# Three buffers of exponentials, banded attention in pairs of blocks, and a half-precision output projection in a hybrid decoder layer

## The chip, the cores and the metric

The kernel runs on one core of a Trainium2 chip. The metric is device time in microseconds (us) of one execution. Engine names are those of the profile: PE multiplies matrices (PEld is its weight load), DVE works on vectors, ACT evaluates functions, POOL is the general engine, SP issues transfers.

## The reference

One decoder layer over 2048 tokens of width 1024 with two attention branches that share one normalised input and one input projection:

```
h    = rms_norm(x, g_pre) * (1 + scale) + shift          # scale, shift, gate from c
proj = h @ w_in  ->  qa ka va fa za (branch A)  qb kb vb zb (branch B)
A: 8 heads of 64, causal softmax attention over all keys, with cumulative
   log-forget gates added to the scores ("FoX")
B: 8 query heads, 2 key heads, rotary positions, window of 128 keys,
   a learned sink logit per head
oa, ob = A * silu(za), B * silu(zb)
y    = concat(oa, ob) @ w_out
out  = x + gate * rms_norm(y, g_post)
```

The inputs and the output are float32. The kernel therefore splits most operands into a high and a low half-precision part and multiplies high x high, high x low and low x high into one sum.

## The kernel before, in words

The order of the work on every engine is written out by hand (`tc.manual_schedule`). Each engine runs its own instructions in the order in which the code issues them. Two helpers spread the work. `fill(n)` issues the next n *units*: a unit is usually three PE products (high x high, high x low, low x high of one slice of 128 rows of the contraction). `after(k, f)` puts f aside, and the k-th call of `tick()` issues it: so an evacuation by ACT or DVE is issued some units after the PE work that it reads. `tick2()` ticks at every second call.

1. *Start* (to about 150 us): modulation vectors from c, normalisation of x, its transpose `hT` in two f16 parts.
2. *Banded stage* (branch B, about 156 to 450 us). 64 `Window` objects, one for each pair of query heads j (4) and block of 128 queries i (16). For each: `scores` (PE, six products 64 rows high, the two heads side by side, L822, into a PSUM tile of one buffer), `maxima` (DVE, L834, which also writes the masked scores to SBUF; POOL copies the sink beside them), `exps` (ACT, L843, two of 257 columns), `turn` (PE, four float32 transposes, L852; ACT and DVE then form the halves, L861 and L857) and `pv` (PE, twelve products, L870; DVE scales them, POOL stores to `o_d`). Between these the loop places the units of the input projection: 296 units over the 64 windows. The four steps of a window are spread over the turns of the loop: scores(n+1) are in the middle of turn n, its transposes at the start of turn n+2.
3. *FoX stage* (branch A, to about 1083 us). Heads 0 to 7, each in 20 *steps* of up to 1024 columns (two key blocks by 512 queries; steps on the diagonal are narrower). Step s: `exp32` (ACT, L1211, reads the scores in PSUM, writes a float32 tile from pool `fxp`, two buffers), `high` (ACT, L1215, f16 copy in a tile from `fxh`, four buffers), `low` (DVE, L1218, the remainder, issued a step later), the scores of step s+1 (PE, L1204 to L1207, one PSUM tile), and `pv` of step s-2 (PE, L1228 to L1231). Between them stand units of the input projection (heads 0 to 6), and `munits`: products and DVE maxima that bound the scores of the next queries (L1156, L1159, L1161), with `ext` rows through PE and ACT (L1123, L1124).
   In head 7 there is no input projection left. Steps 0 to 7 load w_out in 16 pieces, two a step (L1279, from a pool of three buffers), and steps 1 to 8 split them (ACT L1285, DVE L1286) into `wohl`. From step 8 on the first two blocks of the output run as filler (36 units, `N_IN`).
4. *Output* (to the end). 16 blocks of 128 tokens, class `Out`: `turn` in two halves (four transposes each, L1309; DVE multiplies by the gate z, L1313; ACT makes the high part, L1314; DVE the low part, L1315), `product` (three PE products for each of 8 slices and two column halves, L1328), an evacuation (ACT squares, L1337; DVE scales, L1338), and `store` (root of the mean square by DVE, L1347 and L93 to L107; scaling and adding x, L1353; store, L1354). Here both operands are of type float32r, split as high and low of that type.

Of the kernel before, what the change touches and what calls it, by code (L numbers as in the profile page):

```python
# [11 lines left out]
F32R = mybir.dt.float32r  # L12
# [7 lines left out]
P = 128  # L20
S = 2048
D = 1024
# [19 lines left out]
def hybrid_layer(  # L42
# [66 lines left out]


# [38 lines left out]
    snk = const.tile([P, 8], F32, name="snk")  # L149
    mz = const.tile([1, 1], F32, name="mz")  # L150
# [102 lines left out]
    scl, isc, czs, facs, kaps = {}, {}, {}, {}, {}  # L253
# [4 lines left out]
    def w_done(key):  # L258
# [13 lines left out]
        elif kind == "va":  # L272
            kaps[key] = kappa(pw, key)
        else:
            czs[key] = col(f"cz_{key}")
            V.tensor_scalar(czs[key][:], pw[:], pH[:], 2.0 ** -29, op0=ALU.mult, op1=ALU.mult)
            facs[key] = col(f"fac_{key}")
            V.tensor_tensor(facs[key][:], kaps["vb" if kind == "zb" else f"va{j}"][:], czs[key][:], op=ALU.mult)
# [390 lines left out]
    onp = swa_pool("onp", 4)  # L669
# [136 lines left out]
    class Window:  # L806


        def __init__(self, j, i):
            self.j, self.i, self.g = j, i, j // 2  # L810
            self.k0 = max(i - 1, 0)
            self.w = (i + 1 - self.k0) * P
            self.nk = self.w // P

        def scores(self):
            w, i = self.w, self.i
            self.pss = ps_s.tile([P, 2, CH], F32, tag="s", name="pss")
            q, qo = ab[self.j, i // 4], (i % 4) * P
            for n, (a, b) in enumerate(((0, 0), (0, 1), (1, 0))):
                for h in range(2):  # L820
                    r = slice(64 * h, 64 * h + 64)
                    PE.matmul(self.pss[:, h, :w], q[r, a, qo:qo + P],  # L822
                              kst[self.g][r, b, self.k0 * P:(i + 1) * P], start=(n == 0), stop=(n == 2))

        def maxima(self):
            w, moff = self.w, 2 * P - self.w
# [3 lines left out]
            self.sm_ = sws.tile([P, 2, 2 * P + 1], F32, tag="ss", name="sm_")  # L830
            G.tensor_copy(self.sm_[:, :, w:w + 1], snk2.unsqueeze(2))
            m = sm(2, "b_m")
            for h in range(2):
                V.tensor_tensor_reduce(self.sm_[:, h, :w], self.pss[:, h, :w], bmask[:, moff:], scale=scl[key][:],  # L834
                                       scalar=snk2[:, h:h + 1], op0=ALU.add, op1=ALU.max, accum_out=m[:, h:h + 1])
            self.nb = sm(2, "b_nb")
            V.tensor_scalar(self.nb[:], m[:], -1.0, LIFT, op0=ALU.mult, op1=ALU.add)

        def exps(self):
            w, nb_ = self.w, self.nb  # L840
            self.rs = sm(2, "b_rs")
            for h in range(2):
                A.activation(self.sm_[:, h, :w + 1], self.sm_[:, h, :w + 1], AF.Exp, bias=nb_[:, h:h + 1],  # L843
                             accum_out=self.rs[:, h:h + 1])

        def turn(self):

            nk = self.nk
            px = ps_t.tile([P, 4, P], F32, tag="t", name="pxb")
            for h in range(2):  # L850
                for b in range(nk):
                    PE.transpose(px[:, h * nk + b, :], self.sm_[:, h, b * P:(b + 1) * P], ident[:])  # L852
            self.ptt = ptp.tile([P, 8, P], F16, tag="pt", name="ptb")
            hi, lo = self.ptt[:, 0:2 * nk, :], self.ptt[:, 2 * nk:4 * nk, :]

            def low():
                V.tensor_tensor(lo, px[:, 0:2 * nk, :], hi, op=ALU.subtract)  # L857
                self.rinv = sm(2, "b_ri")
                V.reciprocal(self.rinv[:], self.rs[:])

            after(2, lambda: A.activation(hi, px[:, 0:2 * nk, :], AF.Copy))  # L861
            after(3, low)

        def pv(self):
            nk, j, i = self.nk, self.j, self.i
            po = ps_pv.tile([P, 2, 64], F32, tag="pv", name="pob")
            for h in range(2):
                for b in range(nk):
                    for n, (pp_, vv) in enumerate(((0, 0), (0, 1), (1, 0))):
                        PE.matmul(po[:, h, :], self.ptt[:, (pp_ * 2 + h) * nk + b, :],  # L870
                                  vb[:, self.k0 + b, self.g, 64 * vv:64 * vv + 64],
                                  start=(b == 0 and n == 0), stop=(b == nk - 1 and n == 2))

            def out_():
                on = onp.tile([P, P], F32, tag="on", name="on")
                V.tensor_tensor(on[:].rearrange("p (h d) -> p h d", h=2), po[:],
                                self.rinv[:].unsqueeze(2).broadcast_to([P, 2, 64]), op=ALU.mult)
                G.dma_start(o_d[i // 4][(i % 4) * P:(i % 4 + 1) * P, (4 + j) * P:(5 + j) * P], on[:])
# [128 lines left out]
    windows = [Window(j, i) for j in range(4) for i in range(NB)]  # L1007
# [20 lines left out]
    with swa_order:  # L1028
        fill(N_PRO - 4, tick2)
        psx.close()  # L1030
        sws = swa_pool("sws", 2)
        ptp = swa_pool("ptp", 3)
        ps_s = swa_pool("ps_s", 1, space=PSUM)
        ps_t = swa_pool("ps_t", 2, space=PSUM)
        ps_pv = swa_pool("ps_pv", 1, space=PSUM)
        base = N_PRO
# [470 lines left out]
```

## Time and profile before

| | us |
|---|---|
| median of 3 runs (lowest to highest) | 1257.84 (1255.56 to 1259.09) |
| the profiled execution | 1254.68 |
| span of its profile | 1252.9 |
| PE busy | 1192.8 (95%) |
| DVE busy | 911.0 (73%) |
| ACT busy | 677.6 (54%) |
| POOL busy | 154.9 (12%) |

Busy time says how long an engine had an instruction in work; matmuls overlap, so a busy PE can still be spaced wider than it could be. A row of the order of time has start, duration, engine, source line, operation, what it writes and reads with its shape, how many were merged (x6), and in brackets how long the engine idled before it and what released it. Starts of successive PE rows tell the true spacing. In the list of waits the numbers are the total, the count and the longest.

### The profile page before, as it was taken

The page shows a single profiled execution, that of the slowest core. Times are in us where ns is not written, and L with a number is a line of the kernel's source. Part 1 is how long each engine was busy: PE and PEld are TensorE (multiplying, and loading weights), DVE is VectorE, ACT ScalarE, POOL GpSimd, SP SyncE. Part 2 cuts the span into 40 slices and gives each one's busy share as a digit, 9 for nine tenths or more (in the row PEclk, how much of TensorE's full clock was granted, in tenths as well). Part 3 has the DMA queues.
Part 4 walks back from the last instruction along what each step waited for, and adds up shares of the span by engine and source line. Part 5 has one row for each costly group of instructions (what it writes and reads, how often), then busy time and mean ns, then how long its engine had stood idle before and what let it go on. Part 6 is the DMA issues. An engine that isn't in the chain of part 4 may idle for free.

```text
span 1252.9 us, 27686 instructions
## 1 busy us (share of the span) xinstructions
PE 1192.8 (95%) x11042; PEld 772.6 (62%) x11042; DVE 911.0 (73%) x2312; ACT 677.6 (54%) x1085; POOL 154.9 (12%) x284
## 2 busy tenths in 40 slices
PE   6789999999999999999999999999999869999997
PEld 2466546765568966555555555555555547788885
DVE  6867567686777638778888888878777886556554
ACT  2666345455555432675767676676767776322121
POOL 2001123333333310010100100010000000000000
PEclk9899999999999999999999999999999969999999
DMA  9555322213221322232142322132111163355552
GB/s 326 177 145 145 78 80 55 60 56 75 66 80 44 40 65 70 55 104 56 56 58 69 90 66 65 43 77 47 33 39 41 39 189 124 113 202 166 170 169 84
DMA packets 83092, 116.36 MB, mean 93 GB/s; under 512 B 26988, under 2 KB 58772, under 8 KB 82964
## 3 DMA queue, kind: packets, MB, share of 16 engines
q1 hardware_dynamic: 71476, 81.58, 21.5%
q0 software_dynamic: 11488, 33.03, 10.9%
q8 instruction: 86, 1.41, 0.6%
q14 instruction: 42, 0.34, 0.1%
HBM read 67.37 MB, written 25.18 MB: 74 GB/s over the span
## 4 chain that ended last, share of the span: by engine, by line
PE 76%; DVE 9%; DMA 6%; ACT 4%; SPq 3%; issue 2%; POOL 0%; DVEq 0%; ACTq 0%; POOLq 0%
PE bk L298 27%; PE bk L1328 14%; PE bk L316 7%; PE sta L1204 4%; PE sta L1205 4%; PE bk L1156 4%; PE pxb L852 2%; PE poa L1230 2%; PE poa L1231 2%; PE poa L1228 2%; PE pss L822 2%; PE pob L870 2%; DVE pha L1218 2%; ACT p L1211 1%; DMA qs<-qf 1%
## 5 line engine op out<-in xcount | busy, mean ns | idle before, releaser
L1211 ACT ACTIVATE p<-sta,lift,scl_qk 128x1024 f32<-128x1024 f32 (+2 forms) x160 | 172.0, 1075 | 132.7 <-DVE pha L1218 66.8
L298 PE MATMUL bk<-hT,wh_qk 128*128 128x512 f16 x768 | 195.4, 378 | 0.4 <-ACT T L1124 0.4
L1159 DVE TENSOR_REDUCE a_m<-bk 128x1 f32<-128x512 f32 x192 | 131.0, 687 | 59.2 <-PE bk L1156 57.7
L1218 DVE TENSOR_TENSOR pha<-p,pha 128x1024 f16<-128x1024 f32 (+2 forms) x160 | 169.2, 1057 | 0.4 <-ACT pha L1215 0.3
L1328 PE MATMUL bk<-wohl,oz_wraw 128*128 128x512 f32 x512 | 163.2, 400 | 0.0
L1215 ACT ACTIVATE pha<-p 128x1024 f16<-128x1024 f32 (+2 forms) x160 | 148.4, 928 | 4.3
L1204 PE MATMUL sta<-T 128*128 128x512 f16 (+1 forms) x320 | 113.0, 353 | 16.4 <-ACT p L1211 16.1
L1231 PE MATMUL poa<-vt,pha 128*128 128x65 f16 x1088 | 118.3, 194 | 1.3 <-DVE pha L1218 1.3
L1228 PE MATMUL poa<-vt,pha 128*128 128x65 f16 x1088 | 118.6, 194 | 0.0
L1230 PE MATMUL poa<-vt,pha 128*128 128x64 f16 x1088 | 118.5, 196 | 0.0
L298 PEld LDWEIGHTS <-wh_qk 128*128 128x128 f16 x768 | 72.7, 97 | 72.6 <-issue 1.7
L1205 PE MATMUL sta<-T 69*128 69x512 f16 (+1 forms) x320 | 112.1, 355 | 0.0
L1156 PE MATMUL bk<-T 66*128 66x512 f16 (+2 forms) x320 | 111.5, 356 | 0.7 <-DMA T<-stq 0.5
L1228 PEld LDWEIGHTS <-pha 128*128 128x128 f16 x1088 | 102.9, 98 | 14.7 <-issue 1.4
L1230 PEld LDWEIGHTS <-pha 128*128 128x128 f16 x1088 | 102.3, 98 | 12.1 <-issue 1.1
L1328 PEld LDWEIGHTS bk<-wohl,oz_wraw 128*128 128x128 f32 x512 | 93.6, 190 | 18.3
L1231 PEld LDWEIGHTS <-pha 128*128 128x128 f16 x1088 | 102.2, 100 | 1.4 <-DVE pha L1218 1.4
L1328 PE MATMUL bk<-wohl,oz_whl 128*128 128x512 f32 x256 | 101.5, 396 | 0.9 <-DVE oz_whl L1315 0.9
L298 PE MATMUL bk<-hT,wh_za 128*128 128x512 f16 x384 | 100.4, 378 | 0.0
L316 PE MATMUL bk<-wh_va,hT 128*128 128x128 f16 x1536 | 96.0, 219 | 0.0
L298 PE MATMUL bk<-hT,wh_zb 128*128 128x512 f16 x384 | 94.2, 380 | 1.1 <-DVE wh_zb L242 1.1
L316 PEld LDWEIGHTS <-hT 128*128 128x128 f16 x1536 | 89.1, 98 | 6.9 <-issue 4.5
(664 smaller groups left out, 2086.0 us busy)
## 6 DMA issues: line engine op xcount, KB each, us to landing
wa<-in_w_ada_dram SPq DMA_DIRECT2D x16, 512.0 KB, 10.1
z_d<-tz POOLq DMA_DIRECT2D x32, 256.0 KB, 2.7
T<-stq SPq DMA_DIRECT2D x128, 64.0 KB, 2.0
T<-o_d SPq DMA_DIRECT2D x16, 512.0 KB, 5.0
T<-z_d SPq DMA_DIRECT2D x16, 512.0 KB, 4.0
xr<-in_x_dram SPq DMA_DIRECT2D x16, 512.0 KB, 4.5
out_dram<-yg SPq DMA_DIRECT2D x15, 512.0 KB, 3.0
xt<-in_x_dram SPq DMA_DIRECT2D x12, 512.0 KB, 6.3
```

The costliest lines, as they stand in the source:

```text
L298: PE.matmul(ps, whl[:, a, k, :], hT[ci][:, b, k, :], start=(k == 0 and n == 0), stop=(k == KT - 1 and n == 2))
L316: PE.matmul(ps[:, u * P:(u + 1) * P], hT[ci][:, a, k, u * P:(u + 1) * P], whl[:, b, k, :], start=(k == 0 and n == 0), stop=(k == KT - 1 an ...
L1156: PE.matmul(mx[:, :w], T[0:XM, 0, i * P:(i + 1) * P], T[0:XM, 2, pc * CH:pc * CH + w], start=True, stop=True)
L1204: PE.matmul(self.st[:, o:o + w], T[:, 3, kb_], T[:, 1, qc], start=True, stop=False)
L1205: PE.matmul(self.st[:, o:o + w], T[0:XR, 2, kb_], T[0:XR, 0, qc], start=False, stop=not diag)
L1211: A.activation(self.p32[:, :self.w], self.st[:, :self.w], AF.Exp, scale=scl[f"qk{self.hd}"][:], bias=lift[:])
L1215: A.activation(self.ph[:, 0, :self.w], self.p32[:, :self.w], AF.Copy)
L1218: V.tensor_tensor(self.ph[:, 1, :self.w], self.p32[:, :self.w], self.ph[:, 0, :self.w], op=ALU.subtract)
L1228: PE.matmul(po[:, u, :], ph[:, 0, pq], vt[:, b, hd, 0:65], start=(self.first and n == 0 and u == 0), stop=False)
L1230: PE.matmul(po[:, u, 0:64], ph[:, 0, pq], vt[:, b, hd, 65:VW], start=False, stop=False)
L1231: PE.matmul(po[:, u, :], ph[:, 1, pq], vt[:, b, hd, 0:65], start=False, stop=(self.last and n == len(self.blocks) - 1))
L1328: PE.matmul(py, self.hl[i][:, k, :], w_slot(8 * j + k)[:, cc], start=(k == 0 and m_ == 0), stop=(k == KT - 1 and m_ == 2))
```

## The change

It has four parts that work together.

- **Pairs.** `Window` becomes `Pair`: two neighbouring blocks at a time, 32 in all. Scores, maxima, exponentials, transposes and products with the values are issued for both blocks together; PSUM and SBUF tiles are twice as large with one buffer each (results: two of twice the size instead of four). The loop now issues scores(n+1) at the end of turn n, its maxima and exponentials in turn n+1, and its transposes at the end of turn n+1, right behind `pv` of pair n. The transposes' halves are formed one tick earlier.
- **Sum of squares of w_out.** During the 32 turns SP loads w_out in pieces of 128x256, and ACT squares and sums each. After the last pair DVE adds the sums, PE adds over partitions with a ones-matrix, and DVE forms a scale `wrt` from it.
- **FoX.** `fxp` has three buffers of exponentials, `fxh` three. Two empty units stand before the last `ext`.
- **Output in f16.** w_out and the gated values are split into f16 halves after scaling (w_out by `wsc`, the values by a scale per block from their sum of squares, through ACT, a ones-product on PE and two DVE operations). The w_out pieces are in column-half order, with six buffers, loaded two steps ahead and split in steps 2 to 16. The output blocks are turned in one go of eight transposes. Filler blocks start at step 9 in the order (0, first half), (1, first half), (0, second half), (1, second half). The root has four more small operations and is issued apart from the store. x and y get two buffers each from the start.

The core of the diff:

```diff
+    def root_scale(dst, ss):
+        h = small.tile([P, 1], I32, tag="rs_h", name="sc_h")
+        V.tensor_scalar(h[:], ss.bitcast(I32), 1, None, op0=ALU.logical_shift_right)
+        V.tensor_scalar(dst.bitcast(I32), h[:], -1, 0x5F3759DF + (15 << 23), op0=ALU.mult, op1=ALU.add)
...
-    class Window:
+    class Pair:
...
+            self.blocks = [(i + e, max(i + e - 1, 0), 1 + min(i + e, 1)) for e in range(2)]
...
-            after(2, lambda: A.activation(hi, px[:, 0:2 * nk, :], AF.Copy))
-            after(3, low)
+            after(1, lambda: A.activation(hi, px[:, 0:nt, :], AF.Copy))
+            after(2, low)
...
-    windows = [Window(j, i) for j in range(4) for i in range(NB)]
+    windows = [Pair(j, i) for j in range(4) for i in range(0, NB, 2)]
...
-        sws = swa_pool("sws", 2)
-        ptp = swa_pool("ptp", 3)
+        sws = swa_pool("sws", 1)
+        ptp = swa_pool("ptp", 1)
         ps_s = swa_pool("ps_s", 1, space=PSUM)
-        ps_t = swa_pool("ps_t", 2, space=PSUM)
+        ps_t = swa_pool("ps_t", 1, space=PSUM)
...
             todo = goal - pos[0]
+            part = [todo * (m + 1) // 4 - todo * m // 4 for m in range(4)]
+            tick()
             if n:
-                windows[n - 1].turn()
+                wd.maxima()
+            fill(part[0])
             tick()
             if n:
                 wd.exps()
-            fill(todo // 2)
+            fill(part[1])
+            tick()
+            fill(part[2])
+            tick()
+            fill(part[3])
+            if n:
+                windows[n - 1].pv()
+            wd.turn()
             if n + 1 < NW:
                 windows[n + 1].scores()
-            tick()
-            if n + 1 < NW:
-                windows[n + 1].maxima()
-            fill(todo - todo // 2)
-            if n >= 2:
-                windows[n - 2].pv()
+            if n:
+                A.activation(wsq[n - 1][:], wsq[n - 1][:], AF.Square, accum_out=wss[:, (n - 1) % 16:(n - 1) % 16 + 1])
+            if n == 16:
+                V.tensor_reduce(wst[:, 0:1], wss[:], axis=AX.X, op=ALU.add)
+            wsq[n] = wsp.tile([P, 2 * P], F32, tag="wsq", name="wsq")
+            SP.dma_start(wsq[n][:], w_out0[n // 4 * P:(n // 4 + 1) * P, n % 4 * 2 * P:(n % 4 + 1) * 2 * P])
...
         windows[NW - 1].pv()
         tick()
         tick()
+        A.activation(wsq[NW - 1][:], wsq[NW - 1][:], AF.Square, accum_out=wss[:, 15:16])
+        V.tensor_reduce(wst[:, 1:2], wss[:], axis=AX.X, op=ALU.add)
+        wsum = sm(1, "w_mx2")
+        V.tensor_reduce(wsum[:], wst[:], axis=AX.X, op=ALU.add)
+        pw_ = bk[bank()][:, 0:1]
+        PE.matmul(pw_, ones[:], wsum[:], start=True, stop=True)
+        root_scale(wrt[:], pw_)
...
-    fxp = fxs.enter_context(tc.tile_pool(name="fxp", bufs=2, side="right", reuse_waits="tile"))
-    fxh = fxs.enter_context(tc.tile_pool(name="fxh", bufs=4, side="right", reuse_waits="tile"))
+    fxp = fxs.enter_context(tc.tile_pool(name="fxp", bufs=3, side="right", reuse_waits="tile"))
+    fxh = fxs.enter_context(tc.tile_pool(name="fxh", bufs=3, side="right", reuse_waits="tile"))
...
-    munits.append(ext)
+    munits += [lambda: None, lambda: None, ext]
...
-        oio["w"] = wo.tile([P, 2, KT, D], F32R, name="wohl")
+        oio["w"] = wo.tile([P, 2, KT, D], F16, name="wohl")
+        fm = sm(1, "w_p2")
+        V.tensor_reduce(fm[:], fac8[:], axis=AX.X, op=ALU.max)
+        V.reciprocal(fm[:], fm[:])
+        V.tensor_tensor(ysc[:], wrt[:], fm[:], op=ALU.mult)
+        V.tensor_scalar(wsc[:], fac8[:], ysc[:], None, op0=ALU.mult)
...
+        def turn(self, lag):
+            px = [bk[bank()][:].rearrange("p (k n) -> p k n", k=4) for _ in range(2)]
+            for k in range(KT):
+                PE.transpose(px[k // 4][:, k % 4, :], self.o[:, k * P:(k + 1) * P], ident[:])
...
+            after(1, gate)
+            after(2, squares_)
+            after(lag, scale_)          # PE.matmul(pg, ones, gs), then root_scale
+            after(lag + 1, lambda: A.activation(hi, self.z, AF.Copy, scale=self.sc[:]))
+            after(lag + 2, lambda: V.scalar_tensor_tensor(lo, self.z, self.sc[:], hi, op0=ALU.mult, op1=ALU.subtract))
...
             if n == 1:
-                after(3, self.store)
+                last = self.t == NB - 1
+                after(2 if last else 4, self.root)
+                after(2 if last else 7, self.store)
...
+    for t, n in [(0, 0), (1, 0), (0, 1), (1, 1)] + [(t, n) for t in range(2, NB) for n in range(2)]:
...
+            if q == 2 and nxt:
+                ounits.append(lambda nxt=nxt: outs[nxt].turn(4))
...
-    N_IN = 2 * 18
+    N_IN = 4 * KT + 1
...
+        w_at = {r: [r - 2] if r < 10 else [8, 9] if r == 10 else [r - 1] for r in range(2, 17)}
...
-                npn, fil = N_IN * (r - 7) // (NS - 8) - opos[0], ofill
+                npn, fil = N_IN * (r - 8) // (NS - 9) - opos[0], ofill
...
+            if hd == 7:
+                for m in w_at.get(r, []):
+                    w_out_split(m)
...
-            if hd == 7 and 1 <= r <= 8:
-                w_out_split(2 * r - 2)
-                w_out_split(2 * r - 1)
-            if hd == 7 and r < 8:
-                w_out_load(2 * r)
-                w_out_load(2 * r + 1)
-            if hd == 7 and r in (4, 5):
-                outs[r - 4].load()
-            if hd == 7 and r == 6:
-                outs[0].turn(0)
-                outs[0].turn(1)
+            if hd == 7:
+                for m in (w_at[2] if r == 1 else []) + w_at.get(r + 2, []):
+                    w_out_load(m)
+            if hd == 7 and r in (4, 6):
+                outs[r // 2 - 2].load()
+            if hd == 7 and r in (6, 8):
+                outs[r // 2 - 3].turn(3)
```

More of the change, by code (lines that the diff above doesn't have):

```diff
@@ L668, in hybrid_layer @@
     op_ = swa_pool("op", 3)
-    onp = swa_pool("onp", 4)
+    onp = swa_pool("onp", 2)
     stp = swa_pool("stp", 2)
@@ L815, in scores @@
         def scores(self):
-            w, i = self.w, self.i
             self.pss = ps_s.tile([P, 2, CH], F32, tag="s", name="pss")
[L818 to L823, printed above, removed]
+            q = ab[self.j, self.i // 4]
@@ L825, in maxima @@
+            for e, (i, k0, nk) in enumerate(self.blocks):
+                qo, o = (i % 4) * P, e * 2 * P
+                for n, (a, b) in enumerate(((0, 0), (0, 1), (1, 0))):
+                    for h in range(2):
+                        r = slice(64 * h, 64 * h + 64)
+                        PE.matmul(self.pss[:, h, o:o + nk * P], q[r, a, qo:qo + P],
+                                  kst[self.g][r, b, k0 * P:(i + 1) * P], start=(n == 0), stop=(n == 2))
         def maxima(self):
-            w, moff = self.w, 2 * P - self.w
@@ L827, in maxima @@
             key = f"qb{self.j}"
             snk2 = snk[:, 2 * self.j:2 * self.j + 2]
[L830 to L835, printed above, removed]
@@ L836, in maxima @@
-            self.nb = sm(2, "b_nb")
+            self.sm_ = sws.tile([P, 2, 2, 2 * P + 1], F32, tag="ss", name="sm_")
+            m = sm(4, "b_m")
+            for e, (i, k0, nk) in enumerate(self.blocks):
+                w = nk * P
+                G.tensor_copy(self.sm_[:, e, :, w:w + 1], snk2.unsqueeze(2))
+                for h in range(2):
+                    V.tensor_tensor_reduce(self.sm_[:, e, h, :w], self.pss[:, h, e * 2 * P:e * 2 * P + w],
+                                           bmask[:, 2 * P - w:], scale=scl[key][:], scalar=snk2[:, h:h + 1],
+                                           op0=ALU.add, op1=ALU.max, accum_out=m[:, 2 * e + h:2 * e + h + 1])
@@ L837, in maxima @@
+            self.nb = sm(4, "b_nb")
             V.tensor_scalar(self.nb[:], m[:], -1.0, LIFT, op0=ALU.mult, op1=ALU.add)
         def exps(self):
[L840 to L844, printed above, removed]
-        def turn(self):
[L848 to L854, printed above, removed]
+            self.rs = sm(4, "b_rs")
@@ new lines, in exps @@
+            for e, (i, k0, nk) in enumerate(self.blocks):
+                for h in range(2):
+                    p, c = self.sm_[:, e, h, :nk * P + 1], slice(2 * e + h, 2 * e + h + 1)
+                    A.activation(p, p, AF.Exp, bias=self.nb[:, c], accum_out=self.rs[:, c])
+        def turn(self):
+            nt = self.nt
+            px = ps_t.tile([P, 8, P], F32, tag="t", name="pxb")
+            for e, (i, k0, nk) in enumerate(self.blocks):
+                for h in range(2):
+                    for b in range(nk):
+                        PE.transpose(px[:, self.at[e] + h * nk + b, :], self.sm_[:, e, h, b * P:(b + 1) * P], ident[:])
+            self.ptt = ptp.tile([P, 2, 8, P], F16, tag="pt", name="ptb")
+            hi, lo = self.ptt[:, 0, 0:nt, :], self.ptt[:, 1, 0:nt, :]
@@ L864, in pv @@
         def pv(self):
[L865 to L872, printed above, removed]
@@ L874, in out_ @@
-            def out_():
[L875 to L878, printed above, removed]
+            j, i = self.j, self.i
+            po = ps_pv.tile([P, 4, 64], F32, tag="pv", name="pob")
+            for e, (i_, k0, nk) in enumerate(self.blocks):
+                for h in range(2):
+                    for b in range(nk):
+                        for n, (pp_, vv) in enumerate(((0, 0), (0, 1), (1, 0))):
+                            PE.matmul(po[:, 2 * e + h, :], self.ptt[:, pp_, self.at[e] + h * nk + b, :],
+                                      vb[:, k0 + b, self.g, 64 * vv:64 * vv + 64],
+                                      start=(b == 0 and n == 0), stop=(b == nk - 1 and n == 2))
```

106 lines of the change are left out of this document (61 added, 45 removed).

## The prediction, made before the change was run

> **What bounds the kernel now.** I read the page's totals, then busy time by stage, then in each stage the order of time and the waits.
>
> ```profile
> span 1252.9 us, 27686 instructions
> PE 1192.8 (95%) x11042; PEld 772.6 (62%) x11042; DVE 911.0 (73%) x2312; ACT 677.6 (54%) x1085; POOL 154.9 (12%) x284
> ```
> ```profile
> 156.30:449.60 293.30, 291.56 (x3322) 194.69 (x3322) 209.44 (x691) 142.92 (x384) 94.10 (x186) 1.00 0.26 63
> 493.20:984.00 490.80, 485.15 (x4899) 281.93 (x4898) 398.58 (x875) 335.43 (x378) 35.23 (x57) 1.00 0.26 62
> 984.00:996.60 12.60, 10.00 (x150) 6.68 (x149) 10.98 (x19) 10.41 (x12) 0.54 (x1) 1.00 0.09 34
> 996.60:1036.92 40.32, 28.49 (x245) 17.49 (x242) 34.25 (x65) 30.32 (x39) 0.00 (x0) 0.70 0.54 170
> 1036.92:1078.90 41.98, 40.73 (x451) 30.73 (x448) 24.58 (x39) 26.33 (x34) 0.00 (x0) 1.00 0.24 76
> 1095.06:1236.20 141.14, 141.14 (x665) 116.27 (x664) 81.28 (x212) 30.44 (x72) 0.00 (x0) 1.00 0.49 164
> ```
>
> The columns are the stretch, its length, busy PE, PEld, DVE, ACT and POOL, the granted clock, DMA share and GB/s. PE bounds the banded stage (row 1), FoX heads 0 to 6 (row 2) and the output (row 6): there only PE's own spacing counts. The exception is the first half of head 7, row 4: PE is busy 28.49 of 40.32 us at a clock of 0.70, and DVE is the fullest engine. So the change is worth what it takes off PE's spacing in three stages, plus the waits around row 4.
>
> **Part 1, pairs in the banded stage.** The number of products, transposes and exponentials stays; what falls is how often PE switches between kinds. First a row of the chain of waits, then the order of time on PE:
>
> ```profile
> 123.08 7.14 PE bk L298 x33
> ```
> ```profile
> 272.61 0.64 PE L852 MATMUL pxb<-ident,sm__3666 128*128 128x128 f32 x4
> 273.08 1.46 PE L298 MATMUL bk<-hT,wh_qb 128*128 128x512 f16 x6
> 274.47 0.50 PE L822 MATMUL pss<-kst,stb 64*128 64x256 f16 x6
> 274.90 1.47 PE L298 MATMUL bk<-hT,wh_qb 128*128 128x512 f16 x6
> 276.21 0.51 PE L870 MATMUL pob<-vb,ptb 128*128 128x64 f16 x12
> 276.56 0.63 PE L852 MATMUL pxb<-ident,sm__3722 128*128 128x128 f32 x4
> ```
>
> An f16 product of 512 columns takes 7.14/33 = 0.216 us. Six take 1.295, yet the scores begin 1.39 after the six of 273.08: 0.095 for the switch into half-height products. The six scores run two side by side, three slots of 256 columns, half of 0.216 each: 0.325, yet they hold PE for 0.43, another 0.105. The six products behind them take 1.31, 0.015 over. Four transposes of 128 columns hold 0.47, about 0.035 more than four of the steady 0.109. That is 0.25 per block; 64 blocks become 32 pairs: 32 x 0.25 = **-7.9**. If the switch were paid per block inside a pair too, it is 0.
>
> The price is a longer chain from scores to transposes:
>
> ```profile
> 269.87 0.50 PE L822 MATMUL pss<-kst,stb 64*128 64x256 f16 x6
> 270.53 0.55 DVE L834 CUSTOM_DVE_ANT_0 sm__3722<-pss,bmask,snk 128x256 f32<-128x256 f32 x1 [0.94 <-PE pss L822]
> 273.54 0.50 ACT L843 ACTIVATE sm__3722<-sm__3722,b_nb 128x257 f32<-128x257 f32 x1
> ```
>
> The scores end at 270.37, the second exponential at 274.04, and PE asks for the result at 276.56: chain 3.7, slack 2.5. A pair adds two maxima of 0.55 and two exponentials of 0.50: chain 5.8. PE covers it with the pair's product units, three products or 0.65 each. The code spreads 296 units over 32 pairs, 9.25 each, so 6.0, and with the 24 products with the values (0.35 per twelve, from the rows above) 6.7. The slack falls to about 0.9. When DVE is late the evacuations that free the projections' three banks queue behind its maxima. I take **+1.5** for a few late pairs, bounds 0 and +8 (0.25 in each of 32). The single buffers for scores, transposes and results have most of a pair's time between last read and next write; they cost nothing unless that cover goes, and then the price is this same wait.
>
> The 32 w_out pieces add an ACT square each (128x256, near the 0.50 above, so 16 us on ACT, busy 143 of 293 in row 1) and 32 DMAs in SP's queue. PE waits for neither until the end of the stage, so they are hidden; if ACT were late, the exponentials behind the square would be. POOL issues half as many o_d DMAs, off the path. At the end the sum of squares puts a ones-product into PE's queue:
>
> ```profile
> 449.93 0.62 PE L1123 MATMUL bk<-identh,lq 128*69 128x128 f16 x8
> 451.23 1.53 PE L1123 MATMUL bk<-identh,lq 128*69 128x128 f16 x24 [0.69 <-DVE vt L325]
> 450.43 0.76 DVE L325 SCALAR_TENSOR_TENSOR vt<-bk,vt 128x256 f16<-128x256 f32 x2
> ```
>
> It waits for a square and then two reductions, behind DVE work that ends at 451.19, so until about 451.6, from 449.93. Now PE waits here until 451.23, with eight transposes (0.45) done before. Those and the ones-product (0.25, below) come behind the new wait: **+1.1**, bounds +0.5 and +2. Queued behind it are the first FoX rows.
>
> ```profile
> 579.28 0.59 PE L1204 MATMUL sta<-T 128*128 128x512 f16 x1 [2.10 <-ACT p L1211]
> 579.65 0.63 PE L1205 MATMUL sta<-T 69*128 69x512 f16 x1
> 580.08 0.63 PE L1204 MATMUL sta<-T 128*128 128x512 f16 x1
> ```
>
> Here an idle time of 2.10 is followed by products 0.43 apart, twice 0.216, so a wait of 1.7 may cost some products at half pace, up to 1 us: it lies in the upper bound. The Trainium skill, TensorE: Matmul & The Clock Gate (What's actually happening), has the clock fall only after an idle window of about 3.4 us; by it the new wait costs 1.1 and no more, by the row up to 2. The trace disagrees with the page as far as 2.10 sufficed.
>
> The first pair's maxima come earlier than now, where PE waited for them once:
>
> ```profile
> 165.75 0.50 PE L822 MATMUL pss<-kst,stb 64*128 64x256 f16 x6 [1.74 <-DVE b_m L834]
> ```
>
> **-1.0**, bounds 0 and -1.7. Sum of part 1: **-6.3**.
>
> **Part 2, three buffers of exponentials.** In the stall before 579.28, DVE had two maxima of weights ahead of the subtraction that frees the buffer:
>
> ```profile
> 575.12 1.21 DVE L202 TENSOR_REDUCE w_mx<-wr_za 128x1 f32<-128x1024 f32 x1
> 576.85 1.08 DVE L1218 TENSOR_TENSOR pha<-p,pha 128x896 f16<-128x896 f32 x1
> 578.02 1.20 ACT L1211 ACTIVATE p<-sta,lift,scl_qk 128x1024 f32<-128x1024 f32 x1 [2.61 <-DVE a_ri L1235]
> ```
>
> The exponential starts 0.1 after that subtraction, and the scores after the exponential. With a third buffer it waits for the subtraction one step earlier. What is late next is the product with the values, which needs the same subtraction, but some 2.1 later (exponential 1.20, four score products 0.87). PE is idle 490.80 - 485.15 = 5.65 in row 2, and 0.16 more is hidden in each wait whose predecessor's end is modelled 0.38 long at a spacing of 0.216. I take **-6**, bounds 0 and -7. With three instead of four half-precision buffers ACT waits for the values' product of three steps before, which PE got a step earlier: covered, else it gives part of this back.
>
> **Part 3, head 7.** Now all 16 w_out splits fall into steps 1 to 8, where DVE is fullest, and their loads wait in SP's queue for three buffers. Waits of row 4 (total, times, longest) and the DVE half of a split:
>
> ```profile
> PE sta L1204 <- ACT p L1211: 8.1, 6, 2.4
> ACT wohl L1285 <- DMA wo<-in_w_out_dram: 8.2, 7, 2.4
> PE bk L1123 <- DVE lq L1176: 2.8, 1, 2.8
> ```
> ```profile
> L1286 DVE SCALAR_TENSOR_TENSOR wohl<-wo,fac_za,wohl 128x512 fp32r<-128x512 f32 x8 | 5.8, 748 | 0.1
> ```
>
> About 15 splits lie in row 4 and 7 stay there: 8 x 0.75 = 6.0 off DVE, 0.7 added for four small operations on the scales, so 34.25 - 5.3 = 28.9. At the present share (34.25/40.32) that takes 34.0, so -6.3. With no idle time on DVE it is -11.4; with ACT or the chain scores-exponential as the next bound, 0. I take **-6.5**, near the first, because loads two steps ahead and the two empty units before the last row also take away the DMA waits and the 2.8. Row 3 gains **-1** of its 2.6 idle by the third buffer. In row 5, 9 splits arrive and DVE rises from 30.7 to about 36 of 42, below PE's 40.7; shorter products (96 x 0.013, below) and a turn moved ahead give **-2**. Sum **-9.5**, bounds -1 and -16.
>
> **Part 4, half-precision output.**
>
> ```profile
> 1103.31 0.62 PE L1328 MATMUL bk<-wohl,oz_wraw 128*128 128x512 f32 x2
> ...
> 1105.37 0.62 PE L1328 MATMUL bk<-wohl,oz_wraw 128*128 128x512 f32 x2
> ...
> 1106.06 0.60 PE L1309 MATMUL bk<-ident,T 128*128 128x128 f32 x4
> ...
> 1117.95 0.60 PE L1309 MATMUL bk<-ident,T 128*128 128x128 f32 x4
> ```
> ```profile
> 146.97 0.39 PE L775 MATMUL bk<-nf,ones 128*128 128x128 f32 x2
> 147.19 5.34 PE L298 MATMUL bk<-hT,wh_qb 128*128 128x512 f16 x24
> ```
>
> Nine products in 2.06 are 0.229 each; a block takes 11.89. In f16: 48 x 0.216 = 10.37; eight transposes 0.47 + 4 x 0.109 = 0.91; and a ones-product for the scale. L775's two halves hold PE 0.22; I take 0.25, bounds 0.1 and 0.45. Block 11.53, 0.36 less; 14 blocks **-5.0**.
>
> It holds if the low half of the next block is there in time. Behind the turn come gate, square, scale, high half, low half at the ticks 1, 2, 4, 5, 6, a tick each second unit, 13 units or 8.4 us to the next block. Each runs over 1024 columns, so 1.2 by the rows of 576.85 and 578.02, 5.4 with the scale; on DVE the root and the store (3.0 and 1.2) fall among them. Unit by unit I find the low half 0.3 to 1.4 early; were it late by 0.5 each block: +7 in place of slack.
>
> ```profile
> 1246.03 0.15 DVE L1347 TENSOR_TENSOR y_ss<-y_ss 128x1 f32<-128x1 f32 x1
> ...
> 1248.18 1.42 DVE L1353 SCALAR_TENSOR_TENSOR yg<-yg,y_rs,xr 128x512 f32<-128x512 f32 x2
> ```
>
> The last root is 11 small operations in 2.15, 0.195 each; four more stand there, covered by nothing: **+0.8**.
>
> **Sum.** -6.3 - 6 - 9.5 - 5.0 + 0.8 = -26.0. The profiled execution took 1254.68 (span 1252.9), so 1228.7. It lies 3.2 below the shown median of 1257.84; half of that for the spread of runs gives 1230.
>
> **Rivals.**
> - The engines beside PE keep binding: FoX and head 7 keep nearly all waits, and only switches and f16 pay: -6.3 - 5.0 + 0.8 - 2 = -12.5, about 1244. For it: DVE at 85% in row 4. Against: DVE has 92 us free in row 2.
> - All waits go: -7.9 - 7 - 16 - 6 = -37, about 1219.
> - Slower: the pair's chain outruns PE's 6.7 us, and PE waits at the transposes of each of 31 pairs. Without the 1.5 allowed above the gains are 27.5, so it decides from 27.5/31 = 0.89 us a pair, a mean chain of 7.6. At 1.2 us: 37 - 27.5 = +9.7, about 1266. For it: single buffers and DVE in order. Against: the slack of 2.5 now, of which a pair uses 2.1.
> - The output chain is late each block: +7, about 1237, inside the forecast's range.
>
> **Chances.** Forecast 0.64 (its own range 1219 to 1240), other engines 0.17, all waits gone 0.09, slower 0.08, no effect 0.02. Under 0.3% (3.8 us, about what a measurement of this kernel can tell from no change) I put 0.05, from the last and the near side of the slower rival; slower 0.07; faster 0.88. The range 1216 to 1249 leaves out the slower case, no effect and the far ends.
>
> **What would show it.** Right: groups of 12 scores and a full PE in the banded stage; no PE wait for exponentials in heads 0 to 6; head 7's first half near 34 us at a clock near 1; output products 0.216 apart in blocks of 11.5. Wrong: PE waiting at a pair's transposes or for a low half, or DVE full through all of head 7.

## The result and the profile after

The changed kernel takes 1226.53 us (median of four runs, 1224.11 to 1228.36), the one before 1257.41 (1255.56 to 1259.09): a ratio of 0.9753 with a 95% interval from 0.9731 to 0.9776, 2.5% faster. The forecast was 1230, with a range of 1216 to 1249. The profiled execution of the changed kernel took 1228.36, that of before 1254.68.

The totals of the changed kernel's page, and its busy time by stage (columns as in the prediction). Its stages end where the last values' product of the bands starts, then the first exponential of head 0, those of head 7's steps 0 and 9, the last values' product of head 7, and at the last instruction. The views are cut up to 0.05 us beside these; the table below is not:

```profile
span 1226.6 us, 27817 instructions
PE 1172.1 (96%) x11076; PEld 713.3 (58%) x11076; DVE 911.3 (74%) x2273; ACT 701.2 (57%) x1133; POOL 141.7 (12%) x252
```
```profile
158.20:443.40 285.20, 284.35 (x3334) 198.57 (x3334) 197.93 (x564) 151.41 (x416) 80.25 (x153) 1.00 0.33 80
443.40:486.70 43.30, 41.31 (x384) 26.50 (x380) 26.45 (x79) 13.54 (x26) 3.78 (x6) 1.00 0.20 44
486.70:981.66 494.96, 492.31 (x5044) 287.73 (x5043) 407.33 (x895) 346.22 (x389) 36.41 (x59) 1.00 0.26 61
981.66:1015.61 33.95, 23.83 (x251) 14.94 (x248) 28.62 (x63) 23.79 (x30) 0.00 (x0) 0.75 0.44 127
1015.61:1058.22 42.61, 41.51 (x454) 26.06 (x452) 31.58 (x55) 33.92 (x47) 0.00 (x0) 0.96 0.42 135
1058.22:1223.03 164.81, 158.63 (x809) 80.31 (x805) 111.05 (x337) 49.04 (x95) 0.00 (x0) 0.99 0.52 170
```

Two stretches of before, cut at the same events, that the prediction had cut elsewhere (heads 0 to 6, and the output):

```profile
492.50:996.60 504.10, 495.85 (x5051) 288.90 (x5050) 410.16 (x898) 346.51 (x389) 36.47 (x59) 1.00 0.25 61
1078.71:1249.60 170.89, 165.89 (x783) 136.35 (x779) 97.93 (x263) 34.46 (x82) 0.00 (x0) 1.00 0.48 161
```

| stretch, us | before | after | difference | forecast |
|---|---|---|---|---|
| start to the first scores | 156.3 | 158.2 | +1.9 | not touched |
| banded stage | 293.6 | 285.1 | -8.4 | -7.4 |
| to head 0's first exponential | 42.6 | 43.3 | +0.7 | +1.1 |
| heads 0 to 6 | 504.1 | 495.0 | -9.1 | -7 |
| head 7, steps 0 to 8 | 40.3 | 33.9 | -6.3 | -6.5 |
| head 7, the rest | 41.8 | 42.6 | +0.8 | -2 |
| output | 170.9 | 164.8 | -6.1 | -4.2 |

The start is the same code; over the kernels below it ends between 155.9 and 158.2, so the +1.9 is the spread of executions. Without it the rows add up to -28.5 against a forecast of -26.0: the sum is good to 2.5 us, but not row by row. The rows compare one execution of each kernel. These two are 26.3 apart and the medians 30.9, because the profiled execution of before lies 2.7 below its kernel's median and that of the changed kernel 1.8 above. The place to look at is head 7: its first nine steps came out within 0.2 us of the forecast with DVE busy 28.62 of 33.95, at a clock of 0.75 and not near 1. The waits there (total, times, longest):

```profile
ACT wohl L1328 <- DMA wo<-in_w_out_dram: 8.3, 3, 5.6
PE sta L1239 <- ACT p L1246: 7.0, 3, 5.8
PE bk L1368 <- ACT zj L1364: 1.9, 1, 1.9
```

The forecast said that the DMA waits would go. They are 8.3 us, as the 8.2 of before, now in three waits in the place of seven. In order of time, the rows of DVE, SP's queue, ACT and PE around the longest:

```profile
988.60 0.42 DVE L1272 TENSOR_TENSOR ona<-poa,a_ri 128x256 f32<-128x256 f32 x1
```
```profile
968.01 0.46 SPq L1323 DMA_DIRECT2D wo<-in_w_out_dram  x1
989.05 0.36 SPq L1273 DMA_DIRECT2D o_d<-ona  x1
989.46 2.81 SPq L1323 DMA_DIRECT2D wo<-in_w_out_dram  x3
```
```profile
986.48 1.20 ACT L1246 ACTIVATE p<-sta,lift,scl_qk 128x1024 f32<-128x1024 f32 x1 [0.28 <-PE sta L1240]
993.30 0.72 ACT L1328 ACTIVATE wohl<-wo,wsc 128x512 f16<-128x512 f32 x1 [5.62 <-DMA wo<-in_w_out_dram]
993.93 1.04 ACT L1250 ACTIVATE pha<-p 128x1024 f16<-128x1024 f32 x1
994.87 1.19 ACT L1246 ACTIVATE p<-sta,lift,scl_qk 128x1024 f32<-128x1024 f32 x1
```
```profile
996.11 0.59 PE L1239 MATMUL sta<-T 128*128 128x512 f16 x1 [5.78 <-ACT p L1246]
996.49 0.63 PE L1240 MATMUL sta<-T 69*128 69x512 f16 x1
```

Read it backwards. PE waits 5.78 for step 3's exponential. ACT has that exponential behind the high part of w_out's piece 0, for which it waits 5.62 in its queue. The piece is on its way only since 989.46, because in SP's queue the load stands behind the store of head 6's last attention rows, and that store waits until DVE has made them (988.60). The loop `(w_at[2] if r == 1 else []) + w_at.get(r + 2, [])` loads piece 0 at step 0, ahead of that store (968.01), and again at step 1, behind it; the split at step 2 uses the second copy.

### The profile page after: what moved, and what is told of

Its sections match the earlier page's. It is cut to its first block, busy times and chain, and to the rows that moved or that the text cites. A ratio compares the mean times of both kernels' runs of the same rounds, so it can differ in the third digit from the quotient of the medians.

```text
span 1226.6 us, 27817 instructions
## 1 busy us (share of the span) xinstructions
PE 1172.1 (96%) x11076; PEld 713.3 (58%) x11076; DVE 911.3 (74%) x2273; ACT 701.2 (57%) x1133; POOL 141.7 (12%) x252
## 4 chain that ended last, share of the span: by engine, by line
PE 82%; DVE 6%; DMA 5%; ACT 2%; SPq 2%; issue 2%; POOL 0%; DVEq 0%; ACTq 0%; POOLq 0%
PE bk L307 31%; PE bk L1388 13%; PE bk L325 7%; PE sta L1239 5%; PE sta L1240 5%; PE bk L1191 4%; PE poa L1265 3%; PE poa L1266 2%; PE poa L1263 2%; PE pxb L866 2%; PE pss L833 2%; PE pob L885 2%; PE bk L1158 1%; PE bk L1351 1%; DVE pha L1253 1%
## 5 line engine op out<-in xcount | busy, mean ns | idle before, releaser
L1388 PE MATMUL bk<-wohl,oz 128*128 128x512 f16 x768 | 172.6, 380 | 0.0
L1388 PEld LDWEIGHTS <-oz 128*128 128x128 f16 x768 | 74.7, 100 | 81.6 <-issue 0.7
L325 PE MATMUL bk<-wh_va,hT 128*128 128x128 f16 x1536 | 91.0, 219 | 0.8 <-issue 0.8
L307 PE MATMUL bk<-hT,wh_zb 128*128 128x512 f16 x384 | 89.9, 379 | 1.1 <-DVE wh_zb L251 1.1
L307 PE MATMUL bk<-hT,wh_qb 128*128 128x512 f16 x384 | 87.2, 379 | 0.0
```

Source lines behind the costliest of these rows:

```text
L307: PE.matmul(ps, whl[:, a, k, :], hT[ci][:, b, k, :], start=(k == 0 and n == 0), stop=(k == KT - 1 and n == 2))
L325: PE.matmul(ps[:, u * P:(u + 1) * P], hT[ci][:, a, k, u * P:(u + 1) * P], whl[:, b, k, :], start=(k == 0 and n == 0), stop=(k == KT - 1 an ...
L1388: PE.matmul(py, self.hl[:, i, k, :], w_slot(8 * j + k)[:, cc], start=(k == 0 and m_ == 0), stop=(k == KT - 1 and m_ == 2))
```

## The experiments

The theory: four gains that add up (half the switches, the third buffer, shorter f16 products, the split work spread over head 7), less a new stall in head 7 from loads that are issued late. Rivals stand with each run. Each run is compared with runs of before on its own chip, whose medians lie between 1257.06 and 1258.68. So a difference of 1 us between two changed kernels measured on different chips says little, and the ratios to before say more.

### The third buffer taken away (e1), and alone (e2)

```
after:  fxp bufs=3, fxh bufs=3   ->  bufs=2, bufs=4     (first run)
before: fxp bufs=2, fxh bufs=4   ->  bufs=3, bufs=3     (second run)
```


> The changed kernel with two buffers of float32 exponentials and four of half-precision ones again. Theory: the third buffer alone made heads 0 to 6 shorter (504.1 to 495.0 us from the first exponential of head 0 to the first of head 7), so that stretch goes back to 503 to 505 us, ScalarE's exponentials wait again for VectorE, and the whole time goes from 1226.5 to 1235 to 1237 us. Rival: the waits went because the rows of the maxima were given two more units of lag and VectorE had less to do beside them; then the stretch stays at 495 to 497 us and the time at 1226 to 1229 us.

> The kernel before with three buffers of float32 exponentials and three of half-precision ones and nothing else of the change. Theory: the parts add up, so heads 0 to 6 fall by 9 us to 495 us and head 7 by 0 to 2 us; the whole time goes from 1257.4 to 1246 to 1249 us. Rival: the third buffer gives its gain only beside the other parts (the two idle units, the empty queue of SyncE); then the stretch stays above 500 us and the time at 1253 us or more.

Measured: 1232.61 (0.9795, 0.9773 to 0.9817) and 1248.20 (0.9918, 0.9899 to 0.9937). Heads 0 to 6 and head 7's first nine steps, first without the buffer, then with it alone:

```profile
484.22:988.40 504.18, 495.94 (x5053) 288.87 (x5052) 410.19 (x897) 346.50 (x390) 36.45 (x59) 1.00 0.25 60
988.40:1020.42 32.02, 23.97 (x245) 15.13 (x242) 27.32 (x61) 23.96 (x30) 0.00 (x0) 0.77 0.47 136
```
```profile
492.28:987.29 495.01, 492.36 (x5044) 287.73 (x5043) 407.60 (x895) 346.45 (x390) 36.43 (x59) 1.00 0.26 62
987.29:1029.71 42.42, 30.29 (x247) 18.17 (x244) 35.30 (x67) 30.33 (x38) 0.00 (x0) 0.64 0.51 159
```

The stretch is 504.2 or 495.0 by the two pools alone, in both kernels; the two empty units before the last rows do nothing for it. PE's waits for exponentials in it, without and with the buffer:

```profile
PE sta L1239 <- ACT p L1246: 8.0, 11, 2.1
```
```profile
PE sta L1204 <- ACT p L1211: 1.2, 1, 1.2
```

So 6.8 us went in ten waits, and three short waits of another kind, 1.3 in all, came in their place: 5.5 visible. The 0.16 hidden in each of the ten, as the prediction described, make 1.6 more. Another 1.6 is the clock. Behind the longest wait PE runs at half clock (granted clock 0.50) for 3.41 us, here without the buffer and in the profile of before in the same way:

```profile
571.99:575.40 3.41, 3.41 (x28) 1.78 (x25) 1.55 (x6) 2.28 (x3) 0.46 (x1) 0.50 0.00 0
```

In the kernel of the last experiment below, which has the same two buffers and the same waits (8.0, 11, 2.1), the clock stays at 1.00 and heads 0 to 6 take 502.5 and not 504.1. With the buffer no stretch at half clock is left there. About 0.5 of the 9.2 has no row of its own. The first expectation missed the whole time, 1232.6 and not 1235 to 1237: part of the 9.2 was given back in head 7, whose first nine steps take 32.02 without the buffer and 33.95 with it. PE then arrives earlier at loads that come no earlier. In the old head 7, too, the buffer alone makes these steps longer, 40.3 to 42.4.

### Scores of a pair issued apart (e3)

```
 if n + 1 < NW: windows[n + 1].scores(0)     # block 0 of the next pair
 fill(part[3]); windows[n - 1].pv(); wd.turn()
 if n + 1 < NW: windows[n + 1].scores(1)     # block 1
```


> The changed kernel with the pair's two groups of half-height score products issued apart, a quarter of the pair's fill units between them: 32 more passages of TensorE into half-height products and out of them, nothing else. Theory: the banded stage became shorter because there are half as many passages, 0.095 us in and 0.105 us out; so it becomes 32 x 0.2 = 6.4 us longer, 285.1 to 291 to 292 us, and the whole time 1232 to 1234 us. Rival: it became shorter because VectorE, ScalarE and GpSimd have fewer and larger instructions and buffers come free sooner; then it stays at 285 to 286 us and the time at 1226 to 1228 us.

Measured: 1232.04 (0.9793, 0.9772 to 0.9814), 5.5 above the changed kernel. The stage, and the first group of a pair's scores on PE; the second starts at 306.31:

```profile
157.55:448.09 290.54, 290.54 (x3333) 194.37 (x3332) 198.17 (x564) 152.34 (x415) 79.81 (x153) 1.00 0.32 78
```
```profile
302.44 0.50 PE L834 MATMUL pss<-kst,stb 64*128 64x256 f16 x6
302.87 2.12 PE L307 MATMUL bk<-hT,wh_zb 128*128 128x512 f16 x9
```

PE is never idle, so the 5.4 us (290.5 against 285.1) are PE's own spacing: 5.4/32 = 0.17 us for each passage into half-height products and out again, where the rows of before gave 0.20. The changed kernel's 285.1 hold one wait of 0.8 that this run does not have; without it the products alone are 6.2 wider, 0.19 a passage. The Trainium skill, TensorEngine Tiling (Array Packing), Key Properties, says that a change of the tiling mode drains TensorE and gives no price; the trace agrees that it costs, and the price here is 0.17 to 0.19.

### The exponentials of the pairs issued later (e8), then made twice (e10) and three times (e11)

```
e8:  fill(part[0]); wd.maxima(); fill(part[1]); fill(part[2]); wd.exps()
e10, e11:  for _ in range(1 or 2): A.activation(jk, p, AF.Exp, bias)    # ahead of each real one
```


> The changed kernel with the maxima of the pair's scores a quarter of the fill units later and its exponentials two quarters later. In the changed kernel the last exponential of a pair ends about 2.1 us ahead of its first transpose (0.3 to 4.5 us over the 32 pairs), and a quarter of the units is about 1.55 us. Theory: the chain had room of about 2.1 us a pair, so of the 3.1 us TensorE waits about 1 us in each pair: the banded stage goes from 285 to 311 to 325 us, the time to 1252 to 1266 us, which is the slower rival of the prediction. Rival: the chain has more room than the profile shows, because the exponentials wait in ScalarE's queue and not for the maxima: 285 to 295 us.

> The changed kernel with each exponential of the banded pairs made a second time ahead of the real one, into a tile that nobody reads: 4 x 0.49 = 2.0 us more of ScalarE's work between a pair's maxima and its transposes. Theory: the chain has room of about 2.1 us a pair (0.3 to 2.8), so nothing much is lost yet: 0 to 0.3 us a pair, the banded stage 285 to 295 us and the time 1226 to 1236 us. Rival: the chain was at its edge, and every pair pays the 2.0 us: 340 us or more and 1280 us or more.

> The same with two additional exponentials each: 3.9 us more in each pair's chain. Theory: past the room of 2.1 us each pair waits for the rest, 1.8 us x 32 = 58 us, so 330 to 350 us for the banded stage and 1270 to 1292 us in all, slower than the kernel before, which is what the prediction's slower rival said would happen past 0.89 us of wait in each pair. Rival: other work fills TensorE and the chain spreads over two pairs: below 300 us.

Measured: 1226.11 (0.9758, 0.9738 to 0.9779), 1247.63 (0.9926, 0.9910 to 0.9943) and 1309.65 (1.0417, 1.0395 to 1.0438). The banded stage of the three:

```profile
156.05:441.27 285.22, 284.31 (x3333) 198.57 (x3332) 195.31 (x564) 151.05 (x415) 80.26 (x153) 1.00 0.34 80
```
```profile
156.86:464.42 307.56, 292.64 (x3333) 199.04 (x3333) 195.39 (x564) 213.32 (x543) 80.80 (x153) 0.99 0.31 74
```
```profile
157.10:525.76 368.66, 313.83 (x3333) 204.86 (x3333) 195.97 (x564) 277.15 (x671) 80.42 (x153) 0.95 0.26 62
```

The first theory fell: a later place in the program moved the stage by 0.1 us. Averaged over the 32 pairs, the maxima start 0.2 us after the scores end in both kernels, and the exponentials 0.4 us after the maxima, now 0.7; the gap before the first transpose is 2.2, now 1.9. So DVE and ACT were waiting for their inputs and not held up by the work in front. The time is the one that the rival gave, but not for its reason, a wait in ACT's queue. In this stage a place in an engine's order counts only where the engine is busy up to it.

More work in the chain does count, and both further expectations were missed. With the second exponentials PE pays 22.4/32 = 0.7 us a pair, more than the 0 to 0.3 expected and less than the rival's 2.0. The room of a pair is the 2.2 of the gap, but the chain from the scores' end to the last exponential grew from 4.6 to 7.5, by 2.9 and not by 2.0: the maxima now start 1.0 after the scores and not 0.2. 2.9 - 2.2 fits the 0.7; why DVE comes later was not tried. The third kernel is the slower rival of the prediction, made real: 83.5 us, 61.1/32 = 1.9 a pair beyond the second, with waits of PE for ACT's exponentials of up to 1.3 at a time. It lies 19 us above the 330 to 350 expected, and the clock, which the expectation left out, can account for most of that: at 0.95 over 368.66 us it takes up to 17.

### w_out loaded early (e4)

```
-for m in (w_at[2] if r == 1 else []) + w_at.get(r + 2, []):
+for m in (w_at[2] + w_at[3] if r == 0 else []) + w_at.get(r + 4, []):
```


> The changed kernel with the first three pieces of w_out loaded at head 7's first step, ahead of the store of head 6's last output in SyncE's queue, each later one four steps ahead, and the first piece once and not twice. Theory: ScalarE's wait of 5.6 us for the first piece, TensorE's 5.8 us behind it and the lower clock after it go; VectorE's busy time of 28.6 us is then the bound of the first nine steps, which go from 33.95 to 29 to 31 us, and the whole time from 1226.5 to 1220 to 1223 us. Rival: the first nine steps are held by ScalarE and VectorE in turn, whatever the loads do: 33 to 34 us and 1225 to 1227 us.

Measured: 1223.47 (0.9721, 0.9700 to 0.9742), 3.1 below the changed kernel. Head 7's two parts, and PE's longest wait in the first:

```profile
980.91:1011.05 30.14, 20.68 (x258) 12.82 (x255) 28.38 (x63) 23.53 (x30) 0.00 (x0) 0.93 0.47 143
1011.05:1052.97 41.92, 40.82 (x447) 25.59 (x445) 31.32 (x55) 33.85 (x47) 0.00 (x0) 0.97 0.37 118
```
```profile
PE bk L1368 <- ACT zj L1364: 2.8, 1, 2.8
```

The 5.8 us wait is gone, as the theory said, yet the stretch fell by 3.8 only: DVE is busy 28.38 of 30.14, and the next wait grew, that for the sum of squares of output block 0, from 1.9 to 2.8. The whole time is 0.5 over the expected 1220 to 1223.

### The gate rows early (e6), the low parts on GpSimd (e7), the transposes a step later (e9)

```
e6: outs[t].load(z) at r 1, 2; outs[t].load(o) at r 3, 4          (was both at r 4, 6)
e7: e6 and, for pieces 0 to 7: G.tensor_scalar(raw, raw, wsc); G.tensor_tensor(lo, raw, hi, subtract)
e9: e7 and turn at r 7, 9 (was 6, 8); the 33 units from r 10 over ten steps (was r 9, eleven)
```


> The kernel with the early loads of w_out (1223.5 us), and in it the gate rows z of the first two output blocks loaded at head 7's steps 1 and 2 and their attention rows at steps 3 and 4, before at 4 and 6. Theory: VectorE's wait for z, ScalarE's squares behind it and TensorE's wait of 2.8 us for the sum of squares go, with the lower clock after them; the first nine steps are then bound by VectorE's busy time and go from 30.1 to 28.5 to 29.5 us, and the rest of head 7 falls by 0 to 1 us: 1221 to 1223 us in all. Rival: VectorE's work has no gap left, whatever arrives when: 30 us and 1223 to 1224.5 us.

> The kernel with w_out, z and the attention rows loaded early, and in it the low parts of the first eight pieces of w_out made by GpSimd in two operations, which does nothing in head 7, and not by VectorE. Theory: VectorE's 0.75 us a step bind the first nine steps once the loads are early; without them they fall by 8 x 0.75 = 6 us of VectorE's work, to ScalarE's 24.9 us and the waits between engines: 25 to 28 us, 1218 to 1221 us in all. Rival: GpSimd's operations slow VectorE's down, or the low parts come late for the products: the steps stay at 29 us or more and the time at 1222 us or above.

> The kernel with everything loaded early and GpSimd's low parts (1220.5 us), and in it the transposes of the first two output blocks one step later (steps 7 and 9) and the products of the output spread over ten steps from step 10 and not over eleven from step 9. Theory: TensorE's waits of 1.6 us for the attention rows, 0.6 for the sum of squares, 0.7 and 1.3 behind them each get a step of room: the first nine steps go from 28.8 to 26 to 27.5 us, the other eleven from 41.4 to 41 to 42.5 us, the whole time to 1217.5 to 1219.5 us. Rival: the units are TensorE's work in any place, and what the first steps gain the fuller last ten lose: 1219.5 to 1221.5 us.

Measured: 1222.44 (0.9729, 0.9709 to 0.9750; 1.0 below the kernel with early loads of w_out, but not lower as a ratio, 0.9729 against 0.9721, so no gain of the whole time is shown), 1220.48 (0.9712, 0.9692 to 0.9732) and 1222.08 (0.9727, 0.9710 to 0.9743). The last takes 28.32 and 44.16 us for head 7's two parts; the first two:

```profile
980.81:1009.60 28.79, 20.21 (x258) 12.64 (x255) 28.28 (x63) 23.52 (x29) 0.00 (x0) 0.95 0.50 150
1009.60:1052.27 42.67, 41.57 (x448) 25.81 (x445) 31.31 (x55) 33.83 (x47) 0.00 (x0) 0.95 0.37 116
```
```profile
979.79:1008.62 28.83, 21.27 (x258) 13.36 (x255) 26.42 (x56) 23.42 (x29) 19.21 (x14) 0.91 0.48 150
1008.62:1050.03 41.41, 40.31 (x448) 25.25 (x445) 30.92 (x53) 33.73 (x47) 2.73 (x2) 0.98 0.38 120
```

With z early, DVE has no gap left: 28.28 of 28.79. GpSimd should have taken seven splits of 0.74, 5.2 us, off DVE in these steps; its busy time fell by 1.9 only. Most of the reason, in DVE's groups without and with GpSimd's part:

```profile
L1194 DVE TENSOR_REDUCE a_m<-bk 128x1 f32<-128x512 f32 x14 | 9.2, 682 | 0.0
L1253 DVE TENSOR_TENSOR pha<-p,pha 128x1024 f16<-128x1024 f32 x4 | 4.9, 1215 | 0.0
```
```profile
L1194 DVE TENSOR_REDUCE a_m<-bk 128x1 f32<-128x512 f32 x14 | 9.3, 681 | 0.3 <-PE bk L1191 0.3
L1253 DVE TENSOR_TENSOR pha<-p,pha 128x1024 f16<-128x1024 f32 x4 | 7.1, 1786 | 0.0
```

The subtraction with both inputs in SBUF goes from 1215 to 1786 ns, the reduction out of PSUM stays at 682; with the 896-column form (1082 to 1229) that is 2.7 of the missing 3.3. The Trainium skill, SBUF — State Buffer (Who interferes with whom), says that a VectorE instruction with two SBUF inputs contends with a GpSimd instruction that reads SBUF, and that one with at most one such input, outside VectorE's two-port modes, does not. The trace agrees, unevenly: two subtractions beside GpSimd's own subtraction took 2.14 and 2.08 us, two mostly beside its multiplication 1.54 and 1.38; DVE's multiplication of a PSUM by an SBUF tile kept its 0.68.

The first nine steps stayed at 28.8, near the rival's 29, but a slower DVE is only half of it. DVE is idle for 2.4 us now, 1.6 of it for attention rows, whose load stands 3.8 us in SP's queue until the store of such rows has landed. The whole time came into the theory's range by another way: the 1.3 gained in the other eleven steps is the clock, 0.98 in the place of 0.95. With half of the time at half clock taken off, they last 40.7 in both kernels. The last kernel missed its theory, and its rival by 0.6 us at the upper end: 0.5 us less in the first steps, 2.8 more in the fuller last ones. Of all kernels, the one with early loads and GpSimd's low parts is the fastest, 6 us below the changed kernel (0.9712 against 0.9753).

### Half precision alone (e5)

```
before: wohl and oz F32R -> F16; A.activation(hi, z, Copy, scale=2.0 ** -16); lo = z * 2.0 ** -16 - hi
```


> The kernel before with the output product in half precision and nothing else: w_out's pieces and the gated rows as float16, the rows times a fixed 2^-16 so that they stay finite, without the per-block scale (so the small parts keep fewer digits than in the changed kernel). Theory: the products themselves become shorter, from 0.2326 to 0.2158 us from start to start, and the switches between transposes and products stay; a block goes from 11.89 to 48 x 0.2158 + 8 x 0.109 = 11.23 us, 14 blocks -9.2 us, the 32 products in head 7 up to -1.6 us: the whole time from 1258 to 1247 to 1249.5 us. Rival: the blocks were set by something that both precisions share (the weight loads, the evictions), and the gain came from one round of transposes in the place of two; then the block stays at 11.6 us or more and the time above 1253 us.

This kernel leaves out the per-block scale, so that its small parts lose digits; it stands here for its time alone. Measured: 1245.32 (0.9912, 0.9892 to 0.9932), 1.7 below the expected 1247. The output stage, and the products of one stretch in order of time:

```profile
1078.71:1240.29 161.58, 156.59 (x783) 77.85 (x779) 97.72 (x263) 34.29 (x82) 0.00 (x0) 1.00 0.52 170
```
```profile
1102.28 0.38 PE L1328 MATMUL bk<-wohl,oz_whl 128*128 128x512 f16 x1
1102.50 0.59 PE L1328 MATMUL bk<-wohl,oz_wraw 128*128 128x512 f16 x2
```

The stage falls by 9.3 (forecast -9.2 for its 14 blocks): 1102.28 to 1102.50 is one product, 0.22, and the mean of all is 0.2158. In the changed kernel the same gain arrives as 6.1, since the scale that f16 needs costs part of it. The start of one block of the changed kernel:

```profile
1100.40 0.28 PE L1368 MATMUL bk<-w_mx,ones 128*128 128x1 f32 x2
1100.54 5.99 PE L1388 MATMUL bk<-wohl,oz 128*128 128x512 f16 x27
1106.36 1.04 PE L1351 MATMUL bk<-ident,T 128*128 128x128 f32 x8
```

The ones-product holds PE for 0.14 (1100.40 to 1100.54). From the second block of the stage on, blocks are 11.37 apart (transposes at 1072.25 and 1106.36, three blocks), 0.52 under 11.89 and 0.14 over the 11.23 of half precision alone, which is the ones-product. 14 of them make 7.3; the first, 12.06 long with a wait of 0.42 in it, and the longer root at the end take back 1.2. With half precision alone the whole time fell by 2.7 more than the stage, 12.0 from median to median. That is the choice of the execution profiled: the two profiled ones, 1254.68 and 1245.32, are 9.4 apart.

## Why the prediction was right

- **Part 1.** Right in kind: 5.4 of the 8.4 us are the passages into and out of half-height products, measured by e3 (0.17 to 0.19 each, forecast 0.20; 32 x 0.25 is 8.0 and not 7.9). The rest fits the other switches (32 x 0.05) and the first pair's wait, but these were not tried by themselves. The +1.5 for late pairs was not needed: PE shows one wait of 0.8 in the stage, and not for a pair. The chain was over-sized: the first transpose of a pair starts on average 6.8 us after the scores' end and 2.2 after the last exponential, so the chain takes 4.6, not 5.8. The slower rival missed by that much, and e10 and e11 show that it was no fancy.
- **Part 2.** The mechanism is shown from both sides. The term was too small: 9.1, beyond its bound, even with the -1 that Part 3 added for row 3. The failing step is that it priced the waits by PE's idle time alone. The 0.16 hidden in each wait was named and not added, 1.6; and the half clock after 579.28, which Part 1 shows for another purpose, was not counted as a cost of these waits, 1.6 more. Visible idle time fell by 5.5, less than the 7 forecast.
- **Part 3.** The number 34.0 was right by luck. DVE's work fell to 28.62, as worked out (28.9). But "loads two steps ahead take away the DMA waits" is the step that failed: the code loads one copy of piece 0 ahead of a store and uses the other. The prediction counted SP's queue as a place where loads wait for buffers and did not ask what each load stands behind. Late loads took 3.8 us of what the stage could give, and it was these that kept DVE's share at 0.84, near the 0.85 on which the 34.0 rests (with the loads early it is 0.94); the wait of 2.8 for the last row did fall, to 0.9. For the rest of head 7 the forecast was -2 and +0.8 came. There the clock was left out: its first 3.54 us run at half clock, which costs 1.8, after PE's wait of 1.9 for the sum of squares.

```profile
1015.61:1019.15 3.54, 3.54 (x26) 2.90 (x24) 3.38 (x6) 3.31 (x5) 0.00 (x0) 0.50 1.01 285
```

  Without it the stretch would take 40.8, 1.0 less than before.
- **Part 4.** The block was over-sized by 0.16, 0.11 of it the ones-product at 0.14 and not 0.25; and the gain of 0.36 a block became 0.52. No low half was late in the output stage, as the unit count had it. The last root grew from 2.15 to 2.9 us, forecast +0.8.
- Errors of both signs, -2.1, -1.9 and -1.0 against +2.8 in head 7's rest and +1.9 in the start, made the sum better than its terms; that is luck too.

## What to carry to other kernels

A load is issued when the instruction ahead of it in its queue lets it go: list the stores that stand between a load and the step that it is for, and load across them. When a buffer takes waits out of one stage, look at what the earlier arrival meets in the next; 1.9 of 9.2 us went back there. Before an instruction's place in the order is costed, ask whether its engine is busy up to that place. A wait of PE has a price beyond its idle time where the clock falls behind it, so read the granted clock of the stretch that follows.

## What was not expected of the hardware

The clock fell after short idle times, and the traces show what goes with it. In all thirteen the granted clock is full or half, and it changes only at whole steps of 3.41 us from its first record. What PE did in one such step goes with the clock of the next. Two steps of the kernel with GpSimd's part, then two of the one without it:

```profile
989.60:993.02 3.42, 1.89 (x40) 1.40 (x37) 3.39 (x8) 3.42 (x6) 3.34 (x3) 1.00 0.62 176
993.02:996.43 3.41, 3.41 (x28) 1.76 (x25) 3.41 (x4) 1.62 (x3) 3.33 (x3) 0.50 1.05 307
```
```profile
989.72:993.14 3.42, 2.06 (x23) 1.28 (x21) 3.42 (x8) 3.42 (x5) 0.00 (x0) 1.00 0.75 212
993.14:996.55 3.41, 2.25 (x37) 1.53 (x38) 3.38 (x8) 2.02 (x4) 0.00 (x0) 1.00 1.13 315
```

In the first, waits of 0.91 and 0.62 fall into one step, PE is busy 1.89 of 3.42, and the next step's products stand 0.43 apart, twice 0.216. In the second, waits of 0.90 and even 1.62 are parted by the step's end, and the clock stays. Over all steps at full clock in these traces, PE busy for less than 0.45 of the step was always followed by half clock, for more than 0.60 never; in between both occur. So the length of a single wait does not settle it; the same wait of 2.10 in heads 0 to 6 had the fall behind it in the profile of before and not in that of half precision alone.

GpSimd needs 1.60 and 1.16 us for a split's low part of 128x512, which DVE makes in one operation of 0.74.
